# Hybrid decoder step: row tiles 4 to 7 of the input transposed by DMA, three column tiles multiplied while it arrives

## The chip, the core and the metric

The kernel runs on one NeuronCore of a Trainium2 chip as one launch. The metric is the device time of one execution in microseconds (us); shown is the median of three runs. The engines named below are TensorE (PE; PEld is its weight loading), VectorE (DVE), ScalarE (ACT), GpSimd (POOL) and SyncE (SP), which here only issues DMAs. Each engine takes its own instructions strictly in order.

## The reference, cut to what matters

All tokens (1024 prompt rows and 32 sample rows, 2048 wide) are RMS-normalised and multiplied by one wide input projection; attention, a chunked gating branch and an output projection follow and are untouched here.

```python
def _branch_inputs(x, pos, norm_g, w_in, ln_g, ln_b):
    z = _rms_norm(x, norm_g) @ w_in
    q, k, v, ga, u, vc, gb = jnp.split(z, SPLITS, axis=-1)
    ...
    vc = _layer_norm(jax.nn.gelu(vc), ln_g, ln_b)
    return q, k, v, ga, u, vc, gb
```

The part at issue is `x` (float32), its norm, its transposed copy, and the first eight of the 56 column tiles of `w_in`, which make `vc` after a gelu.

## The kernel before, in words

Every float32 operand is split into two float16 halves, a hi part and what it leaves (lo). A product is three matmuls: `xh*wh`, `xl*wh`, `xh*wl`. `xh` and `xl` hold the normalised input with the 2048 features on partitions (16 k-tiles of 128) and the 1056 rows along the free dimension; both stay in on-chip memory.

The input comes in nine row tiles (`TILES`): tiles 0 to 7 have 128 rows, tile 8 is the 32 sample rows. For each tile `x_load` issues one 1 MB DMA into a ring of three `xn` buffers; `x_ss` takes the sum of squares on ACT (one pass over 2048 columns) and the reciprocal root on DVE and POOL; `x_norm` scales the tile on DVE in four pieces of 512; `x_tr` transposes four k-tiles at a time on TensorE into one PSUM bank and `hilo` copies that bank out, hi on ACT and lo on DVE. Four `x_tr` make a tile.

While the input arrives, the kernel multiplies column tiles 0 and 1 of `w_in` row tile by row tile: `proj_chunk(m, t0, n)` issues 48 matmuls (16 k-tiles times three) of 128 columns into one of three PSUM banks (`ps_p`), and `vc_evac` takes the bank through six small steps that go back and forth between ACT and DVE (`gelu2`, L208 to L212, then `hilo`). A bank is free after the second DVE step. Once all rows are there, `run_m` multiplies column tiles 2 to 7 in chunks of 352 rows (`CHUNKS`), 144 matmuls each. A weight tile is two loads of 512 KB into three `wraw` buffers (`w_load`), split into `wh` and `wl` by `w_split` in four parts on ACT and DVE.

All DMAs go through SP's one queue, in order, so a DMA that waits for its operand holds up every later one. The order on each engine is not that of the source: a scheduler in the framework moves instructions between the lines, so the order is shown below as it was built. From column tile 8 on (attention, gating, output projection) the order is the same in both kernels.

Of the kernel before, what the change touches and what calls it, by code (L numbers as in the profile page):

```python
# [15 lines left out]
D = 2048  # L16
# [38 lines left out]
def hybrid_step_kernel(  # L55
# [75 lines left out]

    def w_split(m, part):
        if m >= NIN + NOUT:
            return
        if part == 0:
            w_hl[m] = (
                wp.tile([128, KT, 128], F16, tag="wh", name="wh"),
                wp.tile([128, KT, 128], F16, tag="wl", name="wl"),
            )
# [86 lines left out]
    xp = pool("xp", st, bufs=2)  # L226
# [3 lines left out]
    def x_load(i):  # L230
        t0, n = TILES[i]
        t = xp.tile([128, D], F32, tag="xn", name="xn", bufs=3)
        for hh in range(2 if i == 0 else 1):
            c = slice(hh * 1024, hh * 1024 + 1024) if i == 0 else slice(0, D)
            SP.dma_start(out=t[0:n, c], in_=x[t0:t0 + n, c])
        xn[i] = t
# [17 lines left out]
    lg = lnp.tile([128, 1024], F32, name="lg")  # L254
    lb = lnp.tile([128, 1024], F32, name="lb")
# [6 lines left out]
    def x_ss(i):  # L262
        t0, n = TILES[i]
        t = xn[i]
        ss = xp.tile([128, 1], F32, tag="ss", name="ss")
        junk = xp.tile([128, D], F16, tag="sqj", name="sqj", bufs=1)
        ACT.activation(out=junk[0:n, :], in_=t[0:n, :], func=AF.Square, accum_out=ss[0:n])
        r = xp.tile([128, 1], F32, tag="rr", name="rr")
        rsqrt(r[0:n], ss[0:n], n, 1.0 / D, xp, "ms")
        return r  # L270
# [20 lines left out]

    g2s = {}
# [44 lines left out]
    x_norm(1)  # L337
    for m in range(2):
        g2s[m] = bighl()
    for i in range(NQ + 1):  # L340
        if i + 3 <= NQ:
            x_load(i + 3)
        t0, n = TILES[i]
        for m in range(2):
            if i == 0 and m == 1:
                for part in range(4):
                    w_split(1, part)
            steps = []
            if i < NQ:
                for qd in (2 * m, 2 * m + 1):  # L350
                    steps.append((1.0, lambda qd=qd: x_tr(i + 1, qd)))
# [3 lines left out]
            if m == 0 and i + 2 <= NQ:  # L355
                x_norm(i + 2)
            vc_evac(m, ps, t0, n)
        if i == 2:
            w_load(2)
        if i == 3:  # L360
            w_load(3)
    st.close()


    SP.dma_start(out=lg, in_=ln_g.partition_broadcast(128))
# [32 lines left out]
    for part in range(4):  # L398
        w_split(2, part)
    for m in range(2, 8):  # L400
        g2s[m] = bighl()
        if m == 2:
            steps = vc_trs(0) + vc_trs(1)
# [932 lines left out]
```

## Time and profile before

| | |
|---|---|
| median of 3 runs | 1815.07 us (1813.13 to 1816.42) |
| the profiled execution, its own time | 1817.5 us |
| its span in the trace | 1815.7 us |
| PE / PEld / DVE / ACT busy in the span | 1780.4 / 1223.9 / 1068.4 / 719.6 us |
| DMA moved | 276.13 MB, mean 152 GB/s |

Times in the trace count from the start of the span. A matmul's busy time overlaps that of the next, so the step from one start to the next is its cost, not its duration. DVE and ACT instructions also overlap at their ends by some hundredths of a microsecond, and there too the step between starts is the cost when they follow each other. The number in square brackets at the end of a row is the time that the engine was idle before it, with what ended the wait.

### The profile page before, as it was taken

Reading aid. Unit: us, or ns where it says so; the run is one execution under the profiler, and the core shown is the slowest. Engines: PE = TensorE matmul, PEld = TensorE weight load, DVE = VectorE, ACT = ScalarE, POOL = GpSimd, SP = SyncE. Lnnn points to the kernel's source line nnn. Section 1 sums busy time; section 2 is a strip of 40 time slices with the busy share of each in tenths; the row PEclk is TensorE's granted clock in tenths of the full one; section 3 lists DMA queues with packets and bytes.
Section 4 is the critical chain, followed back from the end, with each engine's and each line's share of the span. In section 5 each row is a group of like instructions: output and inputs, shape, how many; then the busy total and the mean of one; then the engine's idle time right before and its main releaser. Section 6 shows DMA issues by size and latency. Waiting matters only on the chain. (4 is left out here: it accounts for less than half of the span.)

```text
span 1815.7 us, 37262 instructions
## 1 busy us (share of the span) xinstructions
PE 1780.4 (98%) x15040; PEld 1223.9 (67%) x15040; DVE 1068.4 (59%) x2383; ACT 719.6 (40%) x1605; POOL 118.2 (7%) x139
## 2 busy tenths in 40 slices
PE   8999999999999999999999999999999999999997
PEld 7866666666666666666666666666666666666677
DVE  7733595675666576467557657667656633434343
ACT  7522323542543444354344345345345311312133
POOL 0000020110010010001001000001001100000001
PEclk9999999999999999999999999999999999999999
DMA  7343337677667658567657767767765893333314
GB/s 269 105 101 70 77 117 212 147 182 195 159 141 171 163 130 192 152 157 155 168 156 147 168 184 146 177 189 158 186 179 124 233 340 87 70 77 80 78 46 192
DMA packets 340415, 276.13 MB, mean 152 GB/s; under 512 B 255890, under 2 KB 291730, under 8 KB 338130
## 3 DMA queue, kind: packets, MB, share of 16 engines
q1 hardware_dynamic: 340242, 273.76, 59.6%
q8 instruction: 117, 1.92, 0.4%
q14 instruction: 56, 0.45, 0.1%
HBM read 179.85 MB, written 38.26 MB: 120 GB/s over the span
## 5 line engine op out<-in xcount | busy, mean ns | idle before, releaser
L196 PE MATMUL proj<-xh,wh 128*128 128x352 f16 (+3 forms) x3712 | 1108.0, 303 | 3.4 <-DVE ta L495 1.2
L196 PE MATMUL proj<-xl,wh 128*128 128x352 f16 (+3 forms) x3712 | 1107.6, 303 | 1.6 <-DVE xl L154 1.4
L196 PE MATMUL proj<-xh,wl 128*128 128x352 f16 (+3 forms) x3712 | 1107.4, 303 | 0.0
L196 PEld LDWEIGHTS <-wh 128*128 128x128 f16 x7424 | 697.4, 98 | 323.7 <-issue 3.6
L196 PEld LDWEIGHTS <-wl 128*128 128x128 f16 x3712 | 362.7, 98 | 172.3 <-issue 1.9
L146 DVE SCALAR_TENSOR_TENSOR wl<-wraw,wh 128x512 f16<-128x512 f32 x288 | 193.3, 699 | 136.9 <-ACT wh L145 136.9
L145 ACT ACTIVATE wh<-wraw 128x512 f16<-128x512 f32 x288 | 167.2, 620 | 185.9 <-PE proj L196 180.6
L746 DVE SCALAR_TENSOR_TENSOR kvl<-kvr,kvh 128x896 f16<-128x896 f32 x128 | 141.2, 1103 | 67.2 <-ACT kvh L743 51.5
L655 ACT ACTIVATE sp<-sp,mn 128x256 f32<-128x256 f32 (+7 forms) x128 | 99.0, 773 | 161.1 <-DVE mn L643 159.8
L154 DVE SCALAR_TENSOR_TENSOR pn<-sp,pn 128x512 f16<-128x512 f32 (+2 forms) x192 | 111.7, 591 | 66.3 <-ACT pn L153 65.0
L153 ACT ACTIVATE pn<-sp 128x512 f16<-128x512 f32 (+2 forms) x192 | 96.9, 518 | 44.9 <-DMA pt<-pn 38.0
L745 POOL TENSOR_SCALAR kvh<-kvr 128x896 f16<-128x896 f32 x64 | 63.6, 993 | 778.9 <-DVE r L662 343.0
L743 ACT ACTIVATE kvh<-kvr 128x896 f16<-128x896 f32 x64 | 60.5, 945 | 81.1 <-issue 33.9
L643 DVE CUSTOM_DVE_ANT_0 sp<-s,mp 128x512 f32<-128x512 f32 (+3 forms) x128 | 74.5, 582 | 23.2 <-PE s L635 23.2
L682 PE MATMUL o<-vst,pt 128*128 128x128 f16 x576 | 66.3, 220 | 9.1 <-DVE onat L694 8.7
L154 DVE SCALAR_TENSOR_TENSOR yhl<-proj,yhl 128x352 f16<-128x352 f32 (+1 forms) x42 | 21.4, 509 | 82.0 <-ACT yhl L153 82.0
L153 ACT ACTIVATE yhl<-proj 128x352 f16<-128x352 f32 (+1 forms) x42 | 18.8, 447 | 125.2 <-PE proj L196 96.2
L634 PE MATMUL s<-khd,qst 128*128 128x512 f16 (+2 forms) x192 | 62.8, 327 | 1.9 <-DVE mn L643 1.9
L689 PE MATMUL o<-vst,pt 128*128 128x64 f16 x576 | 62.9, 193 | 0.0
L635 PE MATMUL s<-klo,qst 128*128 128x512 f16 (+2 forms) x192 | 60.2, 327 | 0.0
L689 PEld LDWEIGHTS <-pt 128*128 128x128 f16 x576 | 50.5, 98 | 12.4 <-issue 8.5
L682 PEld LDWEIGHTS <-pt 128*128 128x128 f16 x576 | 52.5, 99 | 6.1 <-DMA pt<-pn 2.3
(191 smaller groups left out, 1486.3 us busy)
## 6 DMA issues: line engine op xcount, KB each, us to landing
wraw<-in_w_in SPq DMA_DIRECT2D x110, 512.0 KB, 4.7
kvr<-in_kc SPq DMA_DIRECT2D x64, 448.0 KB, 3.8
kvr<-in_vc SPq DMA_DIRECT2D x64, 448.0 KB, 3.9
wraw<-in_w_out SPq DMA_DIRECT2D x32, 512.0 KB, 5.0
yn<-in_x SPq DMA_DIRECT2D x8, 1024.0 KB, 13.1
out_y_p<-yn SPq DMA_DIRECT2D x16, 512.0 KB, 3.5
xn<-in_x SPq DMA_DIRECT2D x7, 1024.0 KB, 6.9
out_v_o<-tb SPq DMA_DIRECT2D x24, 176.0 KB, 3.8
```

Of the source, the lines that this page charges most:

```text
L145: ACT.activation(out=hi[:, sl, :], in_=r[:, rs, :], func=AF.Copy, scale=WS)
L146: DVE.scalar_tensor_tensor(out=lo[:, sl, :], in0=r[:, rs, :], scalar=WS, in1=hi[:, sl, :], op0=ALU.mult, op1=ALU.subtract)
L153: ACT.activation(out=hi, in_=src, func=AF.Copy, scale=scale)
L154: DVE.scalar_tensor_tensor(out=lo, in0=src, scalar=scale, in1=hi, op0=ALU.mult, op1=ALU.subtract)
L196: PE.matmul(out=ps[:, 0:n], lhsT=a[:, k, :], rhs=b[:, k, c0:c0 + n], start=(i == 0), stop=(i == 3 * KT - 1))
L634: PE.matmul(out=ps[:, 0:n], lhsT=qst[h][:, tq], rhs=khd[h][:, j0:j0 + n], start=True, stop=False)
L643: DVE.tensor_tensor_reduce(sp[:, j0:j0 + n], ps[:, 0:n], mp[:, S - nk + j0:S - nk + j0 + n], 1.0 / (QS * KS), prev, ALU.add, ALU.min, mn,)
L655: ACT.activation(out=sp[:, 0:nk], in_=sp[:, 0:nk], func=AF.Exp, scale=-1.0, bias=prev, accum_out=den)
L682: PE.matmul(out=o[:, 0:128].rearrange("p (l c) -> p l c", l=2), lhsT=pt[:, j], rhs=vst[:, :, kb, h * HD:(h + 1) * HD], start=(kb == 0), st ...
L689: PE.matmul(out=o[:, 0:64], lhsT=pt[:, w + j], rhs=vst[:, 0, kb, h * HD:(h + 1) * HD], start=False, stop=(kb == nb - 1))
L745: POOL.tensor_scalar(hi, r, VS, 1.0, ALU.mult, ALU.mult)
L746: DVE.scalar_tensor_tensor(out=lo, in0=r, scalar=KS if j < DB else VS, in1=hi, op0=ALU.mult, op1=ALU.subtract)
```

## The change

Row tiles 4 to 7 are no longer transposed on TensorE. `x_dma` splits the normalised tile into float16 hi and lo halves while it still lies with rows on partitions (two pieces of 1024 columns, ACT and DVE), and four DMA transposes write them into `xh` and `xl`. Tiles 0 to 3 and the sample tile keep `x_tr`. Three column tiles (`NST = 3`) are multiplied per row tile instead of two, so five are left for `run_m`. The sample tile is taken before row tile 7. Row tile 0 is loaded and squared in four pieces. Buffers: the third column tile's weights live in the pool `xp`, its gelu result and the float16 copies in the buffers `gt`, `lg` and `lb` of the layer norm, which are loaded later for that reason.

```diff
@@ -129,13 +129,16 @@
             )
         w_raw[m, half] = t
 
+    NST = 3
+
     def w_split(m, part):
         if m >= NIN + NOUT:
             return
         if part == 0:
+            wq = xp if m == NST - 1 else wp
             w_hl[m] = (
-                wp.tile([128, KT, 128], F16, tag="wh", name="wh"),
-                wp.tile([128, KT, 128], F16, tag="wl", name="wl"),
+                wq.tile([128, KT, 128], F16, tag="wh", name="wh"),
+                wq.tile([128, KT, 128], F16, tag="wl", name="wl"),
             )
         n = KT // 4
         sl = slice(part * n, (part + 1) * n)
@@ -223,15 +226,15 @@
     right = ExitStack()
     lnp = pool("lnp", right, side="right")
     st = ExitStack()
-    xp = pool("xp", st, bufs=2)
+    xp = pool("xp", st, bufs=1)
 
     xn = {}
 
     def x_load(i):
         t0, n = TILES[i]
         t = xp.tile([128, D], F32, tag="xn", name="xn", bufs=3)
-        for hh in range(2 if i == 0 else 1):
-            c = slice(hh * 1024, hh * 1024 + 1024) if i == 0 else slice(0, D)
+        for hh in range(4 if i == 0 else 1):
+            c = slice(hh * 512, hh * 512 + 512) if i == 0 else slice(0, D)
             SP.dma_start(out=t[0:n, c], in_=x[t0:t0 + n, c])
         xn[i] = t
 
@@ -251,8 +254,6 @@
     gnat = lnp.tile([128, 2, NQ, 1024], F16, name="gnat")
     gsm = lnp.tile([128, 8, NS], F32, name="gsm")
     gnat_s = lnp.tile([NS, 1024], F32, name="gnat_s")
-    lg = lnp.tile([128, 1024], F32, name="lg")
-    lb = lnp.tile([128, 1024], F32, name="lb")
 
     def rsqrt(out, ss, n, scale, tp, tag, eps=EPS):
         a = tp.tile([128, 1], F32, tag=tag, name=tag, bufs=2)
@@ -262,10 +263,17 @@
     def x_ss(i):
         t0, n = TILES[i]
         t = xn[i]
-        ss = xp.tile([128, 1], F32, tag="ss", name="ss")
+        ss = xp.tile([128, 1], F32, tag="ss", name="ss", bufs=2)
         junk = xp.tile([128, D], F16, tag="sqj", name="sqj", bufs=1)
-        ACT.activation(out=junk[0:n, :], in_=t[0:n, :], func=AF.Square, accum_out=ss[0:n])
-        r = xp.tile([128, 1], F32, tag="rr", name="rr")
+        if i == 0:
+            s4 = xp.tile([128, 4], F32, tag="s4", name="s4", bufs=1)
+            for q in range(4):
+                c = slice(q * 512, q * 512 + 512)
+                ACT.activation(out=junk[0:n, c], in_=t[0:n, c], func=AF.Square, accum_out=s4[0:n, q:q + 1])
+            DVE.tensor_reduce(out=ss[0:n], in_=s4[0:n], axis=mybir.AxisListType.X, op=ALU.add)
+        else:
+            ACT.activation(out=junk[0:n, :], in_=t[0:n, :], func=AF.Square, accum_out=ss[0:n])
+        r = xp.tile([128, 1], F32, tag="rr", name="rr", bufs=2)
         rsqrt(r[0:n], ss[0:n], n, 1.0 / D, xp, "ms")
         return r
 
@@ -289,6 +297,22 @@
         src = p.rearrange("p (a b) -> p a b", a=4)[:, :, 0:n]
         hilo(src, xh[:, qd * 4:qd * 4 + 4, t0:t0 + n], xl[:, qd * 4:qd * 4 + 4, t0:t0 + n], XS)
 
+    def x_dma(i):
+        t0, n = TILES[i]
+        t = xn[i]
+        hi, lo = xq.pop(i) if i in xq else xq_new(i)
+        for hh in range(2):
+            c = slice(hh * 1024, hh * 1024 + 1024)
+            hilo(t[:, c], hi[:, c], lo[:, c], XS)
+            for a, b in ((hi, xh), (lo, xl)):
+                SP.dma_start_transpose(out=b[:, hh * 8:hh * 8 + 8, t0:t0 + n], in_=a[:, c])
+
+    def xq_new(i):
+        tags = ("gt", "gt") if i % 2 == 0 else ("lg", "lb")
+        return tuple(lnp.tile([128, D], F16, tag=t, name="xq", bufs=3 if t == "gt" else 1) for t in tags)
+
+    XD = (4, 5, 6, 7)
+    xq = {4: xq_new(4)}
     g2s = {}
 
     def vc_evac(m, ps, c0, n):
@@ -334,34 +358,46 @@
         x_tr(0, qd)
         w_split(0, qd)
     x_load(2)
-    x_norm(1)
+    w_load(2)
+    for part in range(4):
+        w_split(1, part)
     for m in range(2):
         g2s[m] = bighl()
-    for i in range(NQ + 1):
-        if i + 3 <= NQ:
-            x_load(i + 3)
+    g2s[2] = lnp.tile([128, 2, S], F16, tag="gt", name="g2x", bufs=3)
+    order = [0, 1, 2, 3, 4, 5, 6, 8, 7]
+    for e, i in enumerate(order):
         t0, n = TILES[i]
-        for m in range(2):
-            if i == 0 and m == 1:
+        nxt = order[e + 1] if e < NQ else None
+        for m in range(NST):
+            steps = []
+            if nxt is not None and nxt not in XD and (m > 0 if e == 0 else m < 2):
+                d = 2 * (m - 1) if e == 0 else 2 * m
+                for qd in (d, d + 1):
+                    steps.append((1.0, lambda qd=qd: x_tr(nxt, qd)))
+            if e == 0 and m == 1:
+                x_norm(1)
+                x_load(3)
+            if e == 0 and m == 2:
+                w_load(3)
                 for part in range(4):
-                    w_split(1, part)
-            steps = []
-            if i < NQ:
-                for qd in (2 * m, 2 * m + 1):
-                    steps.append((1.0, lambda qd=qd: x_tr(i + 1, qd)))
+                    w_split(2, part)
             set_steps(steps, 5)
             ps = proj_chunk(m, t0, n)
             drain()
-            if m == 0 and i + 2 <= NQ:
-                x_norm(i + 2)
+            if m == 1 and e + 2 <= NQ:
+                x_norm(order[e + 2])
+                if order[e + 2] in XD:
+                    x_dma(order[e + 2])
+                if e > 0 and e + 3 <= NQ:
+                    x_load(order[e + 3])
             vc_evac(m, ps, t0, n)
-        if i == 2:
-            w_load(2)
-        if i == 3:
-            w_load(3)
+        if e == 4:
+            w_load(4)
     st.close()
 
 
+    lg = lnp.tile([128, 1024], F32, tag="lg", name="lg", bufs=1)
+    lb = lnp.tile([128, 1024], F32, tag="lb", name="lb", bufs=1)
     SP.dma_start(out=lg, in_=ln_g.partition_broadcast(128))
     SP.dma_start(out=lb, in_=ln_b.partition_broadcast(128))
 
@@ -396,11 +432,11 @@
         drain()
 
     for part in range(4):
-        w_split(2, part)
-    for m in range(2, 8):
+        w_split(3, part)
+    for m in range(3, 8):
         g2s[m] = bighl()
-        if m == 2:
-            steps = vc_trs(0) + vc_trs(1)
+        if m == 3:
+            steps = vc_trs(0) + vc_trs(1) + vc_trs(2)
         else:
             steps = vc_trs(m - 1)
         run_m(m, steps, lambda ps, c0, n: vc_evac(m, ps, c0, n))
```

The order of SP's queue around the load of row tile 6. Before, `xn_522` to `xn_836` are row tiles 5 to 7, `xn_991` is the sample tile, and the loads of the layer norm's constants and of two weight pieces come ahead of them.

```order
L235 DMA xn_367<-in_x 128x2048
L365 DMA lg_120<-in_ln_g 128x1024
L127 DMA wraw_677<-in_w_in 128x1024
L127 DMA wraw_834<-in_w_in 128x1024
L366 DMA lb_121<-in_ln_b 128x1024
L235 DMA xn_522<-in_x 128x2048
L235 DMA xn_679<-in_x 128x2048
L235 DMA xn_836<-in_x 128x2048
L235 DMA xn_991<-in_x 32x2048
```

In the changed kernel `xn_813` is row tile 5, `xn_1007` row tile 6, `xn_1201` the sample tile and `xn_1387` row tile 7; `xq_122` and `xq_123` are the hi and lo halves of row tile 4, `xq_997` and `xq_998` those of row tile 5.

```order
L238 DMA xn_813<-in_x 128x2048
L308 DMA_TRANSPOSE xh_84<-xq_122 128x8x128
L308 DMA_TRANSPOSE xl_85<-xq_123 128x8x128
L308 DMA_TRANSPOSE xh_84<-xq_122 128x8x128
L308 DMA_TRANSPOSE xl_85<-xq_123 128x8x128
L238 DMA xn_1007<-in_x 128x2048
L238 DMA xn_1201<-in_x 32x2048
L308 DMA_TRANSPOSE xh_84<-xq_997 128x8x128
L308 DMA_TRANSPOSE xl_85<-xq_998 128x8x128
L308 DMA_TRANSPOSE xh_84<-xq_997 128x8x128
L308 DMA_TRANSPOSE xl_85<-xq_998 128x8x128
L238 DMA xn_1387<-in_x 128x2048
```

The loads of row tiles 6 and 7 now stand behind the transposes of row tiles 4 and 5.

ACT's order around the sum of squares of row tile 6 (`sqj`). Before, it stands between two finished evacuations: `ta`, `ta`, `bighl` are the three ACT steps of one chunk.

```order
L210 ACTIVATE ta_669<-tb_670 128x128
L153 ACTIVATE xh_84<-s_707 128x4x128
L153 ACTIVATE bighl_199<-tb_670 128x128
L267 ACTIVATE sqj_902,ss_901<-xn_679 128x2048
L208 ACTIVATE ta_755<-proj_681 128x128
L153 ACTIVATE xh_84<-v_770 128x4x128
```

In the changed kernel `proj_823` is the bank of row tile 2 and column tile 2; its three ACT steps are `ta_872`, `ta_872` and `g2x_210`.

```order
L156 ACTIVATE xq_997<-xn_813 128x1024
L156 ACTIVATE bighl_209<-tb_816 128x128
L211 ACTIVATE ta_872<-proj_823 128x128
L156 ACTIVATE xq_997<-xn_813 128x1024
L275 ACTIVATE sqj_1181,ss_1180<-xn_1007 128x2048
L213 ACTIVATE ta_872<-tb_873 128x128
L156 ACTIVATE g2x_210<-tb_873 128x128
L211 ACTIVATE ta_929<-proj_880 128x128
L275 ACTIVATE sqj_1377,ss_1376<-xn_1201 32x2048
L213 ACTIVATE ta_929<-tb_930 128x128
```

The sum of squares of row tile 6 now stands in the middle of that evacuation, ahead of the step that lets its bank go.

## Rows read from the trace of the kernel before

**Rows 1.** Groups by line and form, DVE, 9.4 to 73.2 us.
```profile
L278 DVE SCALAR_TENSOR_TENSOR xn<-xn,rr,ng 128x512 f32<-128x512 f32 x32 | 22.7, 746 | 2.8 <-POOL rr L260 2.8
L154 DVE SCALAR_TENSOR_TENSOR xl<-s,xh 128x512 f16<-128x512 f32 x16 | 10.9, 680 | 0.0
...
L209 DVE SCALAR_TENSOR_TENSOR tb<-ta,proj 128x128 f32<-128x128 f32 x13 | 3.6, 279 | 0.1
```
**Rows 2.** Timeline of DVE: start us, us, engine, line, operation, tiles, count.
```profile
47.70 1.41 DVE L278 SCALAR_TENSOR_TENSOR xn<-xn,rr,ng 128x512 f32<-128x512 f32 x2
49.02 0.28 DVE L209 SCALAR_TENSOR_TENSOR tb<-ta,proj 128x128 f32<-128x128 f32 x1
49.22 0.68 DVE L154 SCALAR_TENSOR_TENSOR xl<-v,xh 128x512 f16<-128x512 f32 x1
49.82 0.28 DVE L212 SCALAR_TENSOR_TENSOR tb<-ta,proj 128x128 f32<-128x128 f32 x1
...
72.72 0.68 DVE L154 SCALAR_TENSOR_TENSOR xl<-s,xh 128x512 f16<-128x512 f32 x1
```
**Rows 3.** Waits of PE from 0 to 200 us, first and last of four.
```profile
PE proj L196 <- DVE xl L154: 1.4, 2, 1.1
...
PE t L288 <- issue: 0.7, 1, 0.7
```
**Rows 4.** Timeline of PE around four transposes and twelve matmuls.
```profile
33.46 0.61 PE L288 MATMUL t<-eye_t,xn 128*128 128x128 f32 x4
33.91 0.22 PE L196 MATMUL proj<-xh,wh 128*128 128x128 f16 x1
...
34.58 0.61 PE L288 MATMUL s<-eye_t,xn 128*128 128x128 f32 x4
```
**Rows 5.** Timeline of PE: sample rows from 78.40 us, then chunks of 352.
```profile
78.40 0.18 PE L196 MATMUL proj<-xh,wh 128*128 128x32 f16 x1
...
78.93 0.18 PE L196 MATMUL proj<-xh,wh 128*128 128x32 f16 x1
...
94.77 0.31 PE L196 MATMUL proj<-xh,wh 128*128 128x352 f16 x1
...
96.11 0.31 PE L196 MATMUL proj<-xh,wh 128*128 128x352 f16 x1
```
**Rows 6.** Timeline of the start: ACT, DVE and PE on row tile 0.
```profile
6.56 1.91 ACT L267 ACTIVATE sqj<-xn 128x2048 f16<-128x2048 f32 x1 [1.32 <-DMA xn<-in_x]
...
9.49 2.74 DVE L278 SCALAR_TENSOR_TENSOR xn<-xn,rr,ng 128x512 f32<-128x512 f32 x4 [0.74 <-POOL rr L260]
...
10.30 1.11 PE L288 MATMUL t<-eye_t,xn 128*128 128x128 f32 x4 [0.56 <-DVE xn L278]
```
**Rows 7.** The page's group of the nearest larger hi-lo split on DVE.
```profile
L746 DVE SCALAR_TENSOR_TENSOR kvl<-kvr,kvh 128x896 f16<-128x896 f32 x128 | 141.2, 1103 | 67.2 <-ACT kvh L743 51.5
```
**Rows 8.** DMA issues from 39 to 54 us: count, KB each, median us to landing.
```profile
xn<-in_x SPq DMA_DIRECT2D x2, 1024.0 KB, 6.2
```
**Rows 9.** Timeline of SP: two DMA transposes of 256 KB.
```profile
106.34 2.61 SPq L311 DMA_TRANSPOSE gnat<-bighl  x2
```
**Rows 10.** Windows: busy (count) of PE, PEld, DVE, ACT, POOL; PEclk, DMA share, GB/s.
```profile
39.00:46.00 7.00, 6.89 (x109) 6.65 (x107) 5.35 (x14) 5.65 (x14) 0.55 (x1) 1.00 0.45 153
106.00:113.00 7.00, 7.00 (x49) 4.59 (x48) 2.48 (x5) 1.77 (x4) 0.00 (x0) 1.00 0.91 219
127.00:135.00 8.00, 8.00 (x56) 5.27 (x54) 2.96 (x7) 1.93 (x4) 0.00 (x0) 1.00 0.99 200
133.00:135.00 2.00, 2.00 (x15) 1.32 (x14) 0.89 (x2) 0.50 (x1) 0.00 (x0) 1.00 0.85 300
```
**Rows 11.** Timeline of ACT where a row tile is waited for.
```profile
39.00 1.91 ACT L267 ACTIVATE sqj<-xn 128x2048 f16<-128x2048 f32 x1 [1.42 <-DMA xn<-in_x]
```
**Rows 12.** Timeline of PE: a long wait in the attention stage.
```profile
321.07 0.26 PE L682 MATMUL o<-vst,pt 128*128 128x128 f16 x1 [5.75 <-DVE onat L694]
```
**Rows 13.** Windows, the same stretch: columns as in rows 10.
```profile
320.00:325.00 5.00, 3.93 (x15) 2.02 (x15) 3.27 (x11) 3.09 (x9) 0.00 (x0) 0.50 0.76 159
```

## The prediction

> **What bounds the kernel now.** I read the page's shares first: PE is busy for 98% of the span, so over the whole run TensorE is the bound, and work taken off it is worth its own time unless another engine is late where it stood. The change touches only the first 100 us or so (from column tile 8 on the order on every engine is the same), so I then read that stretch alone. A chunk below is one column tile times one row tile; (3,2) is row tile 3, column tile 2.
>
> There the waits view gives PE, the start apart, only 3.7 us in four lines [rows 3]. But DVE is nearly as full. From its first norm at 9.49 us [rows 6] to the last transposed piece of row tile 7, which ends at 73.4 us [rows 2], 63.9 us pass. In it DVE does 36 norm pieces (32 of them in one group), 40 pieces of 512 that write `xl` or `wl`, 39 evacuation steps (three groups of 13) and 8 small ones [rows 1]. The steps from start to start are 0.66 us for a norm piece (1.32 for two), 0.60 for a piece of 512, 0.20 for an evacuation step [rows 2], some 0.1 for a small one: 23.8 + 24.0 + 7.8 + 0.8 = 56.4 us. So DVE took 1.13 times its work; the rest are waits, the largest the reciprocal root on POOL, 2.8 us [rows 1]. TensorE and DVE are level in this stretch, and a count of TensorE's work alone can't give the answer.
>
> **The change, part by part.** I compare the moment at which the third column tile is done, since after it both kernels do the same. Before: the sample rows start at 78.40 us and take 96 matmuls of 0.025 [rows 5], so column tile 2 starts at 80.8; its 144 matmuls of 0.149 [rows 5] take 21.5. That is 102.3 us.
>
> TensorE's own count. Four transposes take 0.45 us (33.46 to 33.91) [rows 4]; 64 of them go: -7.2. A chunk of 48 matmuls of 128 columns takes 48 x 0.67/12 = 2.68 [rows 4], so column tile 2 by row tiles takes 8 x 2.68 + 48 x 0.025 = 22.6 instead of 21.5: +1.1. At the start the sum of squares is one pass of 1.91 us after the last piece has landed [rows 6]; of four pieces only the last, about 0.6 us and its read-out, comes after the landing, so the norm starts about 1.0 us earlier, at 8.5. TensorE's first transpose waited 0.56 us for it [rows 6]: -0.6. If all of TensorE's 3.7 us of waits went too, the third tile would end at 102.3 - 7.2 + 1.1 - 0.6 - 3.7 = 91.9. That is the floor, 10.4 us earlier.
>
> DVE's count. Chunk (5,1) needs the bank of (4,1), so it can't start before the second DVE step of that evacuation. In the order of DVE this step stands behind all nine norms and all splits of the DMA tiles: 36 norm pieces, 28 pieces of 512 (16 `xl`, 12 `wl`, since a third weight tile is split early), 8 pieces of 1024, 41 evacuation steps, 10 small ones. A piece of 1024 does not occur; the nearest is 896 columns at 1.10 us busy [rows 7], which less the overlap of 0.08 (0.68 busy against a step of 0.60 [rows 2]) and for 1024 columns gives an estimate of 1.16. If it went by two pieces of 512 it would be 1.20; I take 1.16. Sum: 23.8 + 16.8 + 9.3 + 8.2 + 1.0 = 59.1 us. At the old ratio of 1.13 that is 66.8, from 8.5 to 75.3. Behind it TensorE still has (5,1), (5,2) and row tiles 6 and 7, eight chunks of 2.68 = 21.4; three chunks of sample rows, 3.6; and 16 transposes of 32 rows, at most 1.8 by rows 4, taken as 1.4. So 75.3 + 26.4 = 101.7, 0.6 us earlier than before. TensorE's gain of 10 us is thus nearly used up by DVE, because the copies of row tiles 4 to 7 are still split there (9.3 us instead of 9.6), while 4 `wl` pieces and the evacuations of a third column tile come ahead in the queue. ACT has less to do than DVE at each of these steps and is not the bound.
>
> The new wait. The load of row tile 6 now stands in SP's queue behind the four transposes of row tile 4. Two DMA transposes occupied SP for 2.61 us [rows 9], 1.3 each. The last needs DVE's second piece of 1024 of row tile 4; up to there DVE has 20 norm pieces, 26 of 512, 2 of 1024, 18 steps and 7 small ones, 35.4 us, by 1.13 at 8.5 + 40.0 = 48.5. So the load is issued at 49.8 and, at 6.2 us to landing [rows 8], is there at 56.0 if the transposes leave it the DMA engines.
>
> What a transpose costs those engines: a weight load of 512 KB took 0.85 x 2.0 = 1.7 us of their time (133 to 135 us), and two such loads with two transposes 0.91 x 7 = 6.4 or 0.99 x 8 = 7.9 us [rows 10]. That leaves 1.5 to 2.3 us for a transpose of 256 KB, against 0.85 for a plain load of this size. Four are 6 to 9 us, and the row tile itself 0.45 x 7 = 3.2 [rows 10]. At 2.3 the load would land near 58.4, at 1.5 at 56.0; I take 57.2.
>
> The Trainium skill (Advanced Engine Details and Errata, section X-Bar Transpose (TRN2)) says that transposing DMAs on this chip run as fast as ordinary ones. By that a transpose would cost 0.85 us, the load would not be held back by the engines, and the sum would be that of the first rival below. The trace does not agree: 1.5 to 2.3.
>
> The sum of squares of row tile 6 stands on ACT inside the evacuation of (2,2), ahead of the step after which the bank of (2,2) goes to (3,2). It takes 1.9 us [rows 11], and about 0.5 passes until DVE has freed the bank: 57.2 + 2.4 = 59.6. DVE would have come there at 8.5 + 1.13 x 42.9 = 57.0. So everything behind is 2.6 us later. Queued behind the waiting ACT step are the evacuations of (2,2) and (3,0) and the halves of row tile 6; TensorE waits for the first. Before, a late row tile already stopped ACT for 1.42 us [rows 11], so the mechanism is there. Row tile 7 has the same form behind the transposes of row tile 5; I add 0.5.
>
> Sum: 101.7 + 2.6 + 0.5 = 104.8 against 102.3, 2.5 us later. Costed at nothing: the DMA transposes of tiles 4 to 7 as such (tile 4 is needed only at (4,0), five chunks or 13 us after its halves are made); the weights of column tiles 3 and 4 (loaded before the queue fills, split while the last row tile is multiplied); the layer norm's constants, now loaded after the input (used periods later). If the first cover went, TensorE would wait for xh and not for a bank.
>
> Against the profiled span of 1815.7 this gives 1818.2, with the 1.8 us around it 1820.0; that execution is 2.4 above the median of 1815.07, and on the median the sum is 1817.5.
>
> **The rivals.** First, the loads come on time: the transposes cost the DMA engines little, and DVE waits less since its instructions are longer and fewer. With a ratio of 1.08: 8.5 + 63.8 + 26.4 = 98.7, or 3.6 us earlier; at 1.13 0.6 earlier; I put it at -3 (-5 to -1). For it: the load of 56.0 is already before DVE's 57.0, so only the sum of squares would hang over. Against it: the POOL waits of rows 1 are one per row tile and stay.
>
> Second, TensorE's count decides: DVE is let off its waits altogether. Zero idle gives 8.5 + 59.1 + 26.4 = 94.0, 8.3 earlier; the floor is 10.4. I put it at -8 (-10 to -5). For it: 98% of PE on the page. Against: no stretch of rows 1 and 2 shows DVE without waits.
>
> Third, the other side: the transposes crowd out the loads. At 2.3 us each row tile 6 lands 1.2 later than I took; row tile 7 follows 0.8 for the sample rows, 9.2 for the transposes of tile 5 and 3.2 of its own, at 71.6, and its evacuation of (3,2) ends at 74.0 where DVE would be at 72 with the delays so far: 2 more. And TensorE then waits over 5 us at (3,2): behind a wait of 5.75 us [rows 12] the granted clock was 0.50 for a 5 us window [rows 13], the lower of its two levels, 1.2 GHz instead of 2.4; up to 3.4 more, partly hidden by DVE's lag. Together 2.5 + 1.2 + 2 + 3.4 = 9.1 (5 to 14) slower. It decides from a transpose of about 2 us upward.
>
> That wait of 5.75 us itself lies in a stage whose order is unchanged; I leave it in both.
>
> **Chances.** Forecast (-1.5 to +6, centre +2.5) 0.47; loads on time 0.20; TensorE's count 0.15; crowded 0.18. A measurement of this kernel tells 0.2%, 3.6 us, from no change. Faster than that: the second rival and 0.08 of the first, 0.23. Slower: the third and 0.13 of the forecast, 0.31. The rest, 0.46, is within it. The range of 8 in 10 leaves out the outer half of the second rival and the outer half of the third: 1815 - 8 to 1815 + 11, 1807 to 1826.
>
> **What would show it.** Right: PE's waits between 45 and 80 us end mostly with DVE `tb`, the longest of 4 to 7 us right before (3,2) with ACT waiting for the DMA of `xn` just before; DVE over 85% busy from 10 to 75 us; column tile 3 starts near 105 us. Wrong at the load: row tile 6 lands before 54 us. Wrong at DVE: column tile 3 starts before 98. Wrong at the cover: PE waits for the DMA of `xh` or `xl`. Wrong as a whole: a difference that arises after column tile 8.

## The result and the profile after

The changed kernel takes 1824.8 us in the median of four runs (1822.3 to 1827.6), the kernel before 1815.7: a ratio of 1.005 (95% interval 1.0037 to 1.0062), 9.1 us slower. The forecast was 1817.5 with 1.5 us faster to 6 slower as its own span; the range reached to 1826. The two profiled executions differ by 4.8 us only, because that of before lay 1.8 above its median and that of after 2.5 below its own; so the sizes of the loss's parts can't be read from this pair alone.

In the input stage the wait of the forecast is there. The view of TensorE's waits, 0 to 200 us (engine, line, releaser: us, times, longest), now has at its head what was not in [rows 3]:

```profile
PE proj L199 <- DVE tb L215: 8.4, 5, 6.0
...
PE proj L199 <- DVE wl L149: 1.9, 3, 1.1
```

The chain behind the 6.0 us, in the timelines (start us, us, what, idle before and its releaser). SP: four transposes of row tile 4, then the loads of row tiles 6 and 8:

```profile
45.61 1.35 SPq L308 DMA_TRANSPOSE xh<-xq  x1
47.01 2.15 SPq L308 DMA_TRANSPOSE xl<-xq  x1
49.26 1.26 SPq L308 DMA_TRANSPOSE xh<-xq  x1
50.62 1.29 SPq L308 DMA_TRANSPOSE xl<-xq  x1
52.00 1.01 SPq L238 DMA_DIRECT2D xn<-in_x  x2
```

ACT, stopped 4.24 us by that load where it was stopped 1.42 in [rows 11]:

```profile
58.35 1.91 ACT L275 ACTIVATE sqj<-xn 128x2048 f16<-128x2048 f32 x1 [4.24 <-DMA xn<-in_x]
60.17 0.19 ACT L275 ACTIVATION_READ_ACCUMULATOR sqj<-xn 128x1 f32 x1
60.26 0.29 ACT L213 ACTIVATE ta<-tb 128x128 f32<-128x128 f32 x1
```

DVE, the step that frees the bank of (2,2), and TensorE, the first matmul of (3,2):

```profile
60.59 0.29 DVE L215 SCALAR_TENSOR_TENSOR tb<-ta,proj 128x128 f32<-128x128 f32 x1
```
```profile
60.93 0.26 PE L199 MATMUL proj<-xh,wh 128*128 128x128 f16 x1 [6.03 <-DVE tb L215]
```

Read from the bottom up: TensorE waits for DVE, DVE for ACT's second evacuation step, this stands behind a sum of squares, and that behind a load issued at 52.0 us. The engine that the wait names, DVE, is late itself. During this wait the clock fell (windows; columns as in [rows 10], PEclk is the third number from the right):

```profile
59.00:66.00 7.00, 5.07 (x49) 5.07 (x49) 4.46 (x11) 6.42 (x12) 1.09 (x2) 0.51 0.92 194
10.00:75.00 65.00, 54.43 (x779) 51.43 (x780) 55.22 (x114) 45.22 (x89) 4.70 (x8) 0.95 0.87 223
```

0.51 is the lower of TensorE's two levels, 1.2 GHz; the records have it from 59.1 to 65.9. DVE is busy for 55.2 of 65 us. The chunks of 352 [rows 5] begin with the fourth column tile here:

```profile
106.62 0.22 PE L199 MATMUL proj<-xh,wl 128*128 128x128 f16 x1
106.67 0.31 PE L199 MATMUL proj<-xh,wh 128*128 128x352 f16 x1
```

So the third column tile is done at 106.7 instead of 102.3 (the trace of before has 102.37), 4.4 us later (forecast 2.5). At the start nothing came of the four sums of squares [rows 6]:

```profile
7.79 0.63 ACT L272 ACTIVATE sqj<-xn 128x512 f16<-128x512 f32 x1 [0.74 <-DMA xn<-in_x]
```
```profile
9.62 2.08 DVE L286 SCALAR_TENSOR_TENSOR xn<-xn,rr,ng 128x512 f32<-128x512 f32 x3 [0.74 <-DMA wraw<-in_w_in]
```

The rest, some 4.7 of the 9.1 us, arises where the order on every engine is the same in both kernels. Counting TensorE's matmuls back from the last one, which pairs them in the two traces, the changed kernel is 4.3 us behind at 110 us, level at 1400 (0.1) and 4.9 behind from 1415 on. In between it gained on this one execution of before, which lost time there: eleven of the twelve runs below gain on it too. So what this pair loses late, it loses at one place. There one difference stands out, ACT near 1403 us, of before and of after:

```profile
1403.09 0.52 ACT L153 ACTIVATE pn<-sp 128x384 f16<-128x384 f32 x1 [1.34 <-DMA pt<-pn]
```
```profile
1406.48 0.52 ACT L156 ACTIVATE pn<-sp 128x384 f16<-128x384 f32 x1 [3.73 <-DMA pt<-pn]
```

ACT came to its wait 1.0 us later and stood there 2.4 us longer, for the same DMA transposes of `pt`, and TensorE, which lost at most 0.5 us at a time there before, waits (waits of PE, 1395 to 1415 us):

```profile
PE o L718 <- DVE onat L730: 3.2, 1, 3.2
```

The DMA view of 1402 to 1405 us of after shows what lies there (40 slices of 0.075 us: busy tenths and GB/s; then packets, MB and share by queue):

```profile
DMA  9979999999990700000000000001000000002999
GB/s 352 341 239 249 263 246 266 300 177 184 58 92 0 219 0 0 0 0 0 0 0 0 0 0 0 0 7 10 7 10 7 10 10 10 10 7 55 276 276 304
...
q1 hardware_dynamic: 834, 0.28, 114.9%
q8 instruction: 1, 0.02, 2.0%
```

One packet of 0.02 MB in an instruction queue (the 219 GB/s at 1403.0; 2.0% of 16 engines' 3 us is 0.95 us of one engine), and from its start the transposes stand nearly still for 1.6 us. The pages of before and of after tell whose instructions these are:

```profile
PE 1780.4 (98%) x15040; PEld 1223.9 (67%) x15040; DVE 1068.4 (59%) x2383; ACT 719.6 (40%) x1605; POOL 118.2 (7%) x139
...
q8 instruction: 117, 1.92, 0.4%
```
```profile
PE 1777.9 (98%) x15264; PEld 1228.7 (67%) x15264; DVE 1072.6 (59%) x2392; ACT 722.7 (40%) x1620; POOL 118.6 (7%) x139
...
q8 instruction: 119, 1.95, 0.4%
```

2 x 15040 instructions of TensorE by 117 packets, and 2 x 15264 by 119, are about 257 each: a packet brings some 256 instructions of TensorE's. The change adds 448, that is 256 + 192, so in the unchanged part every fetch falls beside other work than before. (The Trainium skill, Runtime: NRT & Kernel Launch, section Instruction fetch mechanics, has blocks of 256 instructions, 16 KiB each, which the counts bear out, and calls the cost of going from one to the next mostly hidden; at this place of the trace it isn't.)

### The profile page after: what moved, and what is told of

Read it like the earlier page. It is cut to its first block, busy times and chain, and to the rows that moved or that the text cites. A ratio compares the mean times of both kernels' runs of the same rounds, so it can differ in the third digit from the quotient of the medians.

```text
span 1820.4 us, 37768 instructions
## 1 busy us (share of the span) xinstructions
PE 1777.9 (98%) x15264; PEld 1228.7 (67%) x15264; DVE 1072.6 (59%) x2392; ACT 722.7 (40%) x1620; POOL 118.6 (7%) x139
## 3 DMA queue, kind: packets, MB, share of 16 engines
q8 instruction: 119, 1.95, 0.4%
## 5 line engine op out<-in xcount | busy, mean ns | idle before, releaser
L199 PEld LDWEIGHTS <-wh 128*128 128x128 f16 x7616 | 709.6, 98 | 327.3 <-issue 12.3
L199 PEld LDWEIGHTS <-wl 128*128 128x128 f16 x3808 | 372.5, 98 | 170.3 <-DVE wl L149 2.9
L782 DVE SCALAR_TENSOR_TENSOR kvl<-kvr,kvh 128x896 f16<-128x896 f32 x128 | 141.2, 1103 | 65.9 <-ACT kvh L779 52.2
L156 ACT ACTIVATE pn<-sp 128x512 f16<-128x512 f32 (+2 forms) x192 | 96.8, 518 | 49.4 <-DMA pt<-pn 46.1
L725 PEld LDWEIGHTS <-pt 128*128 128x128 f16 x576 | 50.7, 98 | 13.0 <-issue 9.0
L729 ACT ACTIVATE ot<-o,r 128x64 f32<-128x64 f32 x128 | 38.8, 303 | 45.0 <-PE o L725 44.9
```

What stands on the lines that cost most here:

```text
L156: ACT.activation(out=hi, in_=src, func=AF.Copy, scale=scale)
L199: PE.matmul(out=ps[:, 0:n], lhsT=a[:, k, :], rhs=b[:, k, c0:c0 + n], start=(i == 0), stop=(i == 3 * KT - 1))
L725: PE.matmul(out=o[:, 0:64], lhsT=pt[:, w + j], rhs=vst[:, 0, kb, h * HD:(h + 1) * HD], start=False, stop=(kb == nb - 1))
L782: DVE.scalar_tensor_tensor(out=lo, in0=r, scalar=KS if j < DB else VS, in1=hi, op0=ALU.mult, op1=ALU.subtract)
```

## The experiments

The theories: A (the forecast's, loads late behind the transposes), B (DVE's work sets the end), C (the transposes fill the DMA engines), P (the place of TensorE's instruction fetches costs about half) and N (chance). "Third tile" is the moment at which the third column tile is done in a run's profile, read as above, 102.3 us in the kernel before; it stands on one profile of each run. The diffs show the lines that make the change; helper lines (`lds`, `evs`, `mm`, the tile of zeros `z`) and those marked `...` are left out.

**1. The load ahead of the transposes.** On SP the load of row tile 6 stands before the transposes of row tile 4, that of the sample tile still behind them; the scheduler moved some steps of ACT, DVE and TensorE with them.

```diff
-                if order[e + 2] in XD:
-                    x_dma(order[e + 2])
-                if e > 0 and e + 3 <= NQ:
-                    x_load(order[e + 3])
+                ld = [x_load(j) for j in {1: (4,), 2: (5, 6), 3: (8,), 4: (7,)}.get(e, ())]
+                if order[e + 2] in XD:
+                    with tc.issue_after((ld or [lds[-1]])[-1].ins): x_dma(order[e + 2])
```


> The changed kernel, but the load of row tile 6 stands on SP ahead of the four DMA transposes of row tile 4 instead of behind them. Measured against the changed kernel: there the load was issued at 52.0 us and landed at 58.3, TensorE waited 6.2 us before (3,2), its granted clock was then halved from 59 to 66 us, and column tile 3 started at 106.7 us; 1824.8 us in all. Theory A (the place in SP's queue makes the load late, and the sum of squares behind it stops ACT inside the evacuation that TensorE needs): the load is issued near 45.5 and lands by 53, the wait before (3,2) is under 3 us, no halved clock near 60 us, column tile 3 starts near 102 (4 to 5 earlier), 1819 to 1821 us. Theory B (DVE's own work sets the end, the late load only hides it): the wait moves to later chunks, column tile 3 still starts at 105 to 107, 1823 to 1826 us. Theory C (the DMA engines are taken by the transposes): the load is issued early and still lands after 55, little changes.

1820.0 us, ratio 1.0038 (1.0026 to 1.005); third tile at 103.1. The load was issued at 44.9 and landed at 52.2, and ACT no longer waits:

```profile
52.29 0.26 ACT L211 ACTIVATE ta<-proj 128x128 f32<-128x128 f32 x1
52.45 1.90 ACT L275 ACTIVATE sqj<-xn 128x2048 f16<-128x2048 f32 x1
```

The longest wait of TensorE between 45 and 80 us is 2.1 us; the halved clock shrank to 3.4 us and did not go. Theory A: in the profile the place on SP, with what moved along with it, accounts for 3.6 of the 4.4 us; the medians' intervals overlap with those of the changed kernel. B falls, and C as the main cause too, though the load took 7.3 us.

**2. The load late, the sum of squares out of the way.** Only ACT's and DVE's order changes.

```diff
-                x_norm(order[e + 2])
+                with tc.issue_after(evs[8].ins) if e == 4 else ExitStack(): x_norm(order[e + 2])
```


> The changed kernel, but the sum of squares of row tile 6 is queued on ACT one evacuation later, behind that of (2,2); SP's and TensorE's orders are those of the changed kernel, so the load is as late as there. Theory A: ACT no longer holds the evacuation of (2,2) for the load, the wait before (3,2) falls from 6.2 us to 3 or less, the halved clock near 60 us goes, column tile 3 starts at 102 to 104 instead of 106.7, 1819 to 1822 us. Theory B (DVE's work sets the end): column tile 3 starts at 105 to 107 all the same, 1823 to 1826 us. A miss of A of its own kind would be that the wait moves one chunk on, to the bank that (3,0) frees, with its 6 us and the halved clock: then the load's lateness counts, not the place of the sum of squares.

1823.1 us, ratio 1.0056 (1.0042 to 1.007); third tile at 104.5. The 6 us became three smaller waits:

```profile
PE proj L199 <- DVE tb L215: 6.1, 5, 2.2
```

Half a hit: the stage is 2.2 us shorter in the profile, the time is not. So the lateness counts, not only the place of the sum of squares; where the 2.2 us went in the median was not found.

**3. and 4. Each half of the change alone.** First three column tiles with TensorE's transposes:

```diff
-    XD = (4, 5, 6, 7)
-    xq = {4: xq_new(4)}
+    XD = ()
+    xq = {}
```


> Three column tiles as in the changed kernel, but row tiles 4 to 7 transposed on TensorE as before: no DMA transposes of the input. TensorE has its 64 transposes back (7.2 us); DVE's split is as long (16 pieces of 512 instead of 8 of 1024, 9.6 against 9.3 us). Theory A (the loss comes through the DMA transposes and the loads behind them): no wait over 3 us for row tile 6, no halved clock near 60 us; column tile 3 starts at 102.3 of the kernel before plus 1.1 for the shorter chunks, 103 to 105; 1815 to 1819 us. Theory B (the third column tile's extra work on DVE is the loss, whoever transposes): column tile 3 at 106 or later, 1823 to 1826 us.

1814.1 us, ratio 1.0000 (0.9991 to 1.0009); third tile at 103.5, of the 103 to 105 expected. The windows (columns as in [rows 10]) show TensorE full and DVE with room:

```profile
50.00:60.00 10.00, 10.00 (x167) 9.96 (x165) 7.58 (x19) 6.25 (x17) 0.55 (x1) 1.00 0.10 28
60.00:70.00 10.00, 10.00 (x166) 9.91 (x164) 7.22 (x19) 5.96 (x16) 0.54 (x1) 1.00 0.30 105
```

Then two column tiles with the DMA's transposes:

```diff
-    NST = 3
+    NST = 2
...
-                for qd in (d, d + 1):
+                for qd in range(4) if e == 0 else (d, d + 1):
...
-            w_load(4)
+            w_load(3)
...
-        w_split(3, part)
-    for m in range(3, 8):
+        w_split(2, part)
+    for m in range(2, 8):
```


> Two column tiles while the input arrives, as before, with row tiles 4 to 7 transposed by the DMA as in the changed kernel; here SP has the load of row tile 6 ahead of the transposes of row tile 4. TensorE is 7.2 us lighter than in the kernel before, DVE has 4 pieces of 512 and the evacuations of a third column tile less in its way than in the changed kernel. Theory A (transposes are cheap where no load stands behind them): the third column tile is done 3 to 8 us earlier than the 102.3 of the kernel before, 94 to 99; 1808 to 1813 us. Theory B (DVE's splits of the copies, 9.3 us against 9.6, keep the stage as long): 101 to 104, 1814 to 1818 us. Theory C (the transposes crowd the DMA engines): TensorE waits over 4 us for a late row tile, 1818 us or more.

1819.6 us, ratio 1.0035 (1.0024 to 1.0046); third tile at 107.1, 4.8 later than before. Theories A and B both miss; of C the time holds (over 1818), the wait of over 4 us only in sum. The longest wait is once more an evacuation that stands behind ACT's sum of squares of row tile 6, though that load was issued at 40.0, before any transpose, and landed at 46.1. After it TensorE waits for the copies themselves (timeline of PE):

```profile
50.60 0.22 PE L199 MATMUL proj<-xh,wh 128*128 128x128 f16 x1 [3.66 <-DVE tb L215]
...
54.14 0.27 PE L199 MATMUL proj<-xh,wh 128*128 128x128 f16 x1 [1.02 <-DMA xh<-xq]
...
56.22 0.26 PE L199 MATMUL proj<-xl,wh 128*128 128x128 f16 x1 [1.82 <-DMA xl<-xq]
```

and its clock is halved for 10.2 and 3.4 us. The third column tile costs the input stage 1.2 us and the time nothing (run 3); the half with the DMA transposes loses with three column tiles and with two.

**5. and 6. The fetches moved.** 35 idle matmuls at the start of the changed kernel, 96 behind the input stage of the kernel before; apart from them and the tile of zeros the traces have the same instructions in the same order on every engine. The diff is that of 5.

```diff
...
+    [PE.matmul(out=pz[:, 0:8], lhsT=z, rhs=z[:, 0:8], start=True, stop=True) for _ in range(35)]
```


> The changed kernel with 35 idle matmuls (8 columns, on a tile of zeros, results never read) at the very start, where TensorE waits for its first data; nothing else moves. In the changed kernel's profile a 16 KB instruction fetch of TensorE's falls among the four transposes of pt at 1403 us, those land 2.4 us later than in the kernel before, TensorE waits 3.5 us at 1408 and its granted clock is halved for 6.8 us. The first and second experiments, with as many TensorE instructions, show the same wait (3.2 and 2.9 us); the third and fourth, with other numbers of instructions, and the kernel before do not. Theory P (half of the median's loss is the place where instruction fetches fall, set by how many TensorE instructions come ahead): with 70 instructions more in front the fetches fall about where the kernel before has them, the wait near 1408 is under 1.5 us, no halved clock behind it; 4 to 6 us less, 1817 to 1820 us beside 1814.0 of before; the input stage is as slow as in the changed kernel (column tile 3 near 106.7). Theory N (it is chance, or the DMA transposes' work later on): the wait stays, 1822 to 1825 us.

1818.4 us, ratio 1.0020 (1.0011 to 1.0029), third tile at 106.6 as in the changed kernel. Work was added and the time fell by about 6 us; the interval does not reach that of the changed kernel. ACT's wait for `pt` is 1.95 us, and in PE's waits of 1395 to 1415 us the line is down to

```profile
PE o L718 <- DVE onat L730: 0.3, 1, 0.3
```

> The kernel before with 96 idle matmuls (8 columns, on a tile of zeros, results never read) right behind the sample rows of its input stage, near 81 us; they cost 96 x 0.025 = 2.4 us of TensorE. 192 instructions more put the fetches 192 of 256 instructions earlier, that is 64 later, about where the changed kernel has them. Theory P: the transposes of pt near 1402 land late here too, TensorE waits about 3 us near 1411, perhaps with a halved clock behind it; 1819 to 1823 us instead of 1814.0. Theory N: only the 2.4 us are added, 1816 to 1817 us.

1823.1 us, ratio 1.0044 (1.003 to 1.0058): 7.6 us more. Of these 4.8 lie up to the third tile (107.1), twice the 2.4 expected: the idle matmuls left a gap of their own, and from 85.1 to 88.5 us the granted clock was 0.50 (timeline of PE):

```profile
80.47 2.52 PE L362 MATMUL v<-z 128*128 128x8 f16 x95
83.91 0.18 PE L362 MATMUL v<-z 128*128 128x8 f16 x1 [0.92 <-issue]
```

The other 2.8 come later. The kernel before has the changed kernel's wait now (ACT, then PE's waits):

```profile
1408.11 0.52 ACT L153 ACTIVATE pn<-sp 128x384 f16<-128x384 f32 x1 [3.00 <-DMA pt<-pn]
```
```profile
PE o L682 <- DVE onat L694: 1.7, 1, 1.7
```

Theory P holds in both directions, here with a wait of 1.7 us where about 3 was expected; no halved clock followed. N, with the 4.8 us in place of its 2.4, would be at 1820.3, just outside the interval; what makes it fall is run 5. In this profile TensorE falls back by 1.8 us near 1408 and by 3.3 more near 1470, behind a wait of 1.8 us for `xh` and a halved clock. Runs 1, 3 and 10 have that too (1.7 to 2.0 us), at other places of the fetches; its cause was not looked for.

**7. Plain copies for the transposes.**

```diff
-                SP.dma_start_transpose(out=b[:, hh * 8:hh * 8 + 8, t0:t0 + n], in_=a[:, c])
+                SP.dma_start(out=b[:, hh * 8:hh * 8 + 8, t0:t0 + n], in_=a[:, c].rearrange("p (k n) -> p k n", n=n))
```


> The changed kernel with the 16 DMA transposes of row tiles 4 to 7 replaced by plain DMA copies of the same 256 KB from and to the same tiles: the transposition of these rows is left out, so the rows that come of them are not the reference's. ACT's order is that of the second experiment (the sum of squares of row tile 6 one evacuation later). Theory C (it is the transposition that fills the DMA engines and SP's time): a copy takes 0.85 us of the 16 engines instead of 1.5 to 2.3 and SP 0.3 to 0.6 instead of 1.3, so the load of row tile 6 is issued near 49.5 and lands by 56 instead of 58.8; the waits of TensorE from 45 to 80 us fall from 6.5 us to under 4, column tile 3 starts at 101 to 103 instead of 104.5; 1818 to 1821 us with the late part of the changed kernel. Rival (the bytes cost, not the transposition; the Trainium skill, Advanced Engine Details and Errata, section X-Bar Transpose (TRN2), has transposing DMAs as fast as others): column tile 3 at 104 to 105, 1822 to 1824 us.

1818.6 us, ratio 1.0019 (1.0008 to 1.0029), third tile at 102.1. SP's row tile 4, to be held against the four rows of the changed kernel above:

```profile
45.16 0.72 SPq L308 DMA_DIRECT2D xh<-xq  x1
46.42 0.59 SPq L308 DMA_DIRECT2D xl<-xq  x1
47.11 0.75 SPq L308 DMA_DIRECT2D xh<-xq  x1
47.96 2.09 SPq L308 DMA_DIRECT2D xl<-xq  x1
50.14 0.62 SPq L238 DMA_DIRECT2D xn<-in_x  x1
```

The load leaves 1.9 us earlier, lands at 56.3, and all waits of TensorE from 45 to 80 us are 3.3 us, none over 1.0. The DMA engines are less busy from 45 to 53 us, and move more (windows of the changed kernel, then of this run):

```profile
45.00:53.00 8.00, 8.00 (x145) 7.99 (x144) 8.00 (x17) 5.38 (x13) 0.00 (x0) 1.00 0.91 130
45.00:53.00 8.00, 8.00 (x148) 8.00 (x145) 8.00 (x17) 5.33 (x14) 0.00 (x0) 1.00 0.76 163
```

Theory C's expectation is met in the waits, the third tile and the time; the load is some tenths later than expected and one copy took SP 2.09. So the transposition costs, on SP and in the engines. Against the 104.5 of run 2 the stage gained 2.4 us, not all of it by the transposition: the load of the sample tile and later steps of ACT and DVE stand at other places here. The Trainium skill (Advanced Engine Details and Errata, section X-Bar Transpose (TRN2)) has a transposing DMA as fast as another; this run decides otherwise.

**8. and 9. Only row tiles 6 and 7 by the DMA**, with the loads ahead of them on SP; in 9 the load of row tile 7 too.

```diff
-    XD = (4, 5, 6, 7)
-    xq = {4: xq_new(4)}
+    XD = (6, 7)
+    xq = {}
...
+                ld = [x_load(j) for j in {1: (4,), 2: (5,), 3: (6,), 4: (8, 7)}.get(e, ())]
                 if order[e + 2] in XD:
-                    x_dma(order[e + 2])
-                if e > 0 and e + 3 <= NQ:
-                    x_load(order[e + 3])
+                    with tc.issue_after((ld or [lds[-1]])[-1].ins):
+                        x_dma(order[e + 2])
```
The diff is that of 9; in 8 the loads keep their turns (8 at e = 4, 7 at e = 5).

> Three column tiles while the input arrives, the DMA transposes row tiles 6 and 7 only, and these stand on SP behind the last row tile's load that they could hold up. Against the third experiment (all on TensorE, column tile 3 at 103.5, 1814.1 us) TensorE loses 32 transposes, 3.6 us. Theory A (transposes cost where loads stand behind them, and DVE has room): column tile 3 at 99.5 to 102, no wait over 3 us and no halved clock between 45 and 80 us, 1809 to 1813 us. Theory B (DVE's work sets the end of this stage): column tile 3 at 103 to 105, 1813 to 1817 us.

1816.6 us, ratio 1.0007 (0.9998 to 1.0016), third tile at 105.8: a miss. Row tile 7's load, still behind four transposes, stopped ACT for 2.46 us and TensorE for 4.2, and the clock was halved for 3.4 us.

> As the eighth run (three column tiles, row tiles 6 and 7 by the DMA), but the load of row tile 7 also stands ahead of the transposes of row tile 6 on SP. There that load was issued at 67.4 us, landed at 72.4, ACT stood 2.5 us at its sum of squares, TensorE waited 4.2 us before the next chunk, and column tile 3 started at 105.8; 1816.6 us. Theory A: the load is issued by 64 us, that wait falls under 2 us, column tile 3 starts at 101 to 102.5, 1811 to 1814 us, that is level with or up to 2 us under the kernel before. Rival: the slot of the row tile that it replaces comes free only near 67 us, so the load is as late as there and nothing changes, 1815 to 1818 us.

1813.0 us, ratio 1.0004 (0.9995 to 1.0012), third tile at 103.2. Theory A's size is missed: a wait of 2.4 us stays (4.3 in all, as in 8, but with no halved clock), since that load was issued at 62.4 only, when DVE had read the slot out, and landed at 68.8. It is 0.5% faster than the changed kernel and level with the one before; no version measured beats the latter.

**10. Both repairs.** The diffs of 1 and 5 together.

> The first experiment (load of row tile 6 ahead of the transposes) with the 35 idle matmuls of the fifth run at the start. If the two losses are independent, the input stage has what the first experiment took back (column tile 3 near 103) and the late part what the 35 matmuls took back (no wait over 1.5 us near 1408): 1813 to 1816 us, level with the kernel before. If they share a cause, it is no better than the better of the two, 1818 to 1820 us.

1815.1 us, ratio 1.0017 (1.0008 to 1.0027), third tile at 102.1, waits near 1408 us at most 0.5. Within the expected 1813 to 1816, but its interval overlaps that of run 5, so that the two repairs add up is seen in the profile, not in the time.

**11. Idle matmuls in the long wait**, 163 between (3,1) and (3,2).

```diff
             drain()
+            if e == 3 and m == 1:
+                pz = bank(ps_o, "o")
+                with tc.issue_after(mm[0].ins):
+                    for _ in range(163):
+                        PE.matmul(out=pz[:, 0:8], lhsT=z, rhs=z[:, 0:8], start=True, stop=True)
```


> The changed kernel with 163 idle matmuls (8 columns, zeros, 0.025 us each, 4.1 us) on TensorE between (3,1) and (3,2), that is inside its wait of 6.2 us; 326 instructions more put the late instruction fetches where the 35 matmuls of the fifth run put them (70 and one whole block of 256 more), so it is to be compared with that run, 1818.4 us, column tile 3 at 106.6. If the granted clock fell because TensorE stood idle there, it stays at 1.00 between 59 and 66 us, and of the 3.4 us that the halved clock takes 2 to 3.4 come back: column tile 3 at 103 to 104.5, 1815 to 1817 us. If the wait alone sets the end (TensorE catches up behind DVE anyway), column tile 3 stays at 106 to 107 and the time at 1818 us.

1818.3 us, ratio 1.0039 (1.0026 to 1.0052), third tile at 107.0: nothing came back. The timeline of PE, and the window behind:

```profile
55.76 3.42 PE L391 MATMUL o<-z 128*128 128x8 f16 x131
61.11 1.02 PE L391 MATMUL o<-z 128*128 128x8 f16 x32 [1.94 <-issue]
```
```profile
59.00:66.00 7.00, 5.07 (x79) 4.97 (x76) 3.83 (x10) 6.05 (x11) 0.73 (x2) 0.54 1.24 185
```

The clock fell all the same, after matmuls of 8 columns and a gap of 1.94 us with the releaser "issue": TensorE waited for nothing that the profile shows. Its next instructions are the likely reason (a fetch at 58.4 us took 1.3), as in run 6; no run shows it. What the halved clock alone costs here stays open.

**12. Row tile 0 in two loads, four sums.**

```diff
-        for hh in range(4 if i == 0 else 1):
-            c = slice(hh * 512, hh * 512 + 512) if i == 0 else slice(0, D)
+        for hh in range(2 if i == 0 else 1):
+            c = slice(hh * 1024, hh * 1024 + 1024) if i == 0 else slice(0, D)
```


> The changed kernel with row tile 0 loaded in two pieces of 512 KB as before and still summed in four pieces on ACT; for the start alone (its later order on SP differs by one place, so its time is not compared). In the changed kernel the last of four pieces of 256 KB landed at 7.76 us, against 6.48 for the last of two in the kernel before, and the first norm piece started at 9.62 against 9.49. If cutting the load in four makes it land later: the last piece lands near 6.5 here, the last sum starts at once and the first norm piece starts near 8.5, the 1.0 us that the four sums were to give. If the landing varies by itself: it is 7 us or later here too, and the norm starts at 9.3 or later.

The last piece landed at 6.4 us, the last sum began at 7.09, and the norm at

```profile
8.91 2.74 DVE L286 SCALAR_TENSOR_TENSOR xn<-xn,rr,ng 128x512 f32<-128x512 f32 x4 [0.74 <-POOL rr L261]
```

0.7 us earlier than in the changed kernel, 0.6 earlier than in the kernel before, though not at the 8.5 expected. So the sums were good for 0.6, and the four loads took it away: the last piece landed at 7.2 to 8.3 us in the eleven traces with four, at 6.4 to 6.5 in the three with two. One run, 1819.2 us.

**All runs side by side.** TensorE's instructions beyond those of the kernel before, modulo 256 (twice the difference of the page's counts); the wait for `onat` or another near 1408 us; the median less that of before in the same runs; and what is left when the third tile's delay in the profile is taken off.

| run | mod 256 | third tile | wait | median | left |
|---|---|---|---|---|---|
| changed | 192 | 106.7 | 3.2 | +9.1 | +4.7 |
| 1 | 192 | 103.1 | 2.9 | +6.0 | +5.2 |
| 2 | 192 | 104.5 | 2.6 | +9.1 | +6.9 |
| 7 | 192 | 102.1 | 2.6 | +3.1 | +3.3 |
| 6 (before + 96) | 192 | 107.1 | 1.7 | +7.6 | +2.8 |
| 12 (one run) | 192 | 102.6 | 1.6 | +6.0 | +5.7 |
| 5 | 6 | 106.6 | 0.5 | +2.9 | -1.4 |
| 11 | 6 | 107.0 | 0.5 | +5.1 | +0.4 |
| 10 | 6 | 102.1 | 0.5 | +1.9 | +2.1 |
| 8 | 0 | 105.8 | 0.6 | +1.1 | -2.4 |
| 9 | 0 | 103.2 | 0.5 | -0.2 | -1.1 |
| 3 | 64 | 103.5 | 0.0 | +0.1 | -1.1 |
| 4 | 128 | 107.1 | 0.0 | +5.6 | +0.8 |

The six kernels at 192 have 4.8 us left on the mean (2.8 to 6.9), the seven others -0.4 (-2.4 to 2.1). The last column takes the third tile from one profile each and holds to some 2 us. The traces themselves part more sharply: with the kernel before there are fourteen, and in the six at 192, and in no other, a fetch of TensorE's falls between the issue of the first of the four transposes of `pt` and its landing; there it takes 5.6 to 6.6 us to land, in the eight others 4.2 to 4.9.

## Why the prediction was right in part

- **The sum without the loads, 101.7 us: near.** With the loads earlier the third tile is done at 102.1 to 103.1 (runs 1, 7 and 10). Part of that is luck, since the sum starts at 8.5 us and the first norm at 9.6. That DVE stood level with TensorE was only half so: in run 3 DVE is busy for 7.2 to 7.6 of 10 us and TensorE is full.
- **The late load: right in its mechanism, too small.** Issue, landing, the sum of squares and the chunk (3,2) are those named. Issue was 52.0 for 49.8, landing 58.3 for 57.2, the bank free at 60.9 for 59.6; DVE came to the second step of (4,1) at 79.4 for 78.4, and TensorE needed 27.3 us behind it for 26.4. Together +5.0 stands where +3.1 was put. The four transposes took SP 1.26 to 2.15 us each, not 1.3.
- **The halved clock** was put with the third rival. It came, for 6.8 us; its share in the 5.0 us was not separated.
- **The head, -0.6: wrong.** It came out at +0.1, since the last of four pieces landed at 7.76 and not at 6.48 (run 12).
- **"After it both kernels do the same": the step that failed.** The order was the same and the time was not: what the third tile's delay leaves of the 9.1 us, about 4.7, goes with the place of TensorE's instruction fetches (run 5 took 6 back, 4.8 arise at that place in the profiles). That cost was put at nothing without having been looked at. A difference behind column tile 8 was the prediction's own sign of being wrong as a whole.
- **The rivals.** Loads on time was the kernel of run 7, not this one; TensorE's count never decided. The third rival's 9.1 us is the measured loss to the digit by chance, with other terms: the input stage gave 4.4 of it. That the time lies in the range is luck as well: the forecast's own span ended at 6 us slower, and half of the loss came from where none was looked for.
- **The cover** held: no wait for `xh` or `xl` here. In run 4, with two column tiles, it was gone (2.8 us).

## What to carry to other kernels

A transfer that is added to a queue is priced by what is queued behind it: look for the load that some in-order engine meets inside an evacuation. When a change adds or removes hundreds of instructions, the unchanged rest can move by as much as the change is worth; pad the instruction count both ways before a half-percent result is put down to the edit. And take the two halves of a compound change apart early: here the third column tile was free and the DMA transposes lost.

## What the hardware showed

- A fetch of 256 TensorE instructions fell among DMA transposes in the changed kernel, and these stood nearly still for 1.6 us. 70 idle instructions in front gave 6 us back; 192 in the kernel before cost some 3 beyond what they cost in place.
- Behind 262 instructions for matmuls of 8 columns, run in 3.4 us, came a gap of 1.94 us with the releaser "issue", behind 190 of them in run 6 one of 0.92.
- A DMA transpose of 256 KB took SP 1.23 to 2.48 us in 15 of 16 cases of the changed kernel (5.19 in one), a plain copy 0.59 to 0.75 in 12 of 16 cases of run 7 (1.6 to 2.2 in four).
- Row tile 0 in four pieces of 256 KB was complete 0.7 to 1.8 us later than in two of 512 KB (7.2 to 8.3 against 6.4 to 6.5 us).
